# The beginning of a hybrid decoder block: a weight piece in four transfers, norm weights turned on TensorE, transposes by halves between matmuls

## Chip, cores and metric

One core of a Trainium2 chip runs the kernel. The metric is the device time of one execution in microseconds; lower is better. The kernel before was timed in three runs, the median is 810.13 us.

## What is computed

The block takes 512 tokens of 1024 float32 features. The part that matters here is its first step: an RMS norm with weights `norm1_g`, then one projection with `w_in` into 4096 columns.

```python
h = rmsnorm(x, norm1_g)          # x * rsqrt(mean(x*x) + EPS) * g
proj = h @ w_in                  # (512, 1024) @ (1024, 4096)
u, q, k, v, gate_p, gate_a = columns of proj
x = x + (sigmoid(gate_p) * pool_mixer(u) @ w_pool_up
         + sigmoid(gate_a) * diff_attention(q, k, v) @ w_attn_up) @ w_out
x = x + hier_moe(rmsnorm(x, norm2_g))   # top 1 of 4 groups, top 2 of 8 experts in it, 32 SwiGLU experts
```

The expert weights are by far the largest input: 32 experts of three 1024 x 512 float32 matrices.

## The kernel before, in words

**Tiles.** The 512 tokens are four tiles of 128. `w_in` is cut into pieces of 512 rows by 512 columns (1 MB, four chunks of 128 rows, `k` = 0 to 3). Pieces 0 and 1 are the two row halves of the query columns, 2 and 3 those of the key columns, and so on. A product at the precision wanted is three matmuls: high part by high part, high by low and low by high. So every weight chunk is split by `split_to` (lines 149 to 167): ScalarE multiplies the chunk by the norm weights and rounds it to the high part `wh` (line 159), VectorE forms the rest `wl` (line 160). The activations are treated in the same way: `h_transpose` (line 257) transposes the normed token tile on TensorE into the PSUM tile `tx` (line 262, 128 columns at a time), ScalarE copies it to the high part `hTh` (line 265), VectorE forms `hTl` (line 266). Half 0 of `hT` belongs to the first 512 features and so to even pieces, half 1 to odd ones.

**A unit.** `tok_unit` (line 270) is one piece by one token tile: for each of four chunks the matmuls of lines 274, 275 and 276, twelve in all. It can call a function after a chunk (`mid`).

**Order.** The schedule is written out by hand: each engine carries out its instructions in the order in which the program issues them, and waits only on what it reads or overwrites. The beginning is lines 466 to 485. First twelve matmuls of the identity (line 469, tile `warm`) keep TensorE busy while x arrives. Then `h_norm` of tiles 0 and 1 (sum of squares on ScalarE, line 250; mean plus EPS on VectorE, line 252; power -0.5 on GpSimd, line 188; scaling on VectorE, line 254), the transposes of tile 0, two chunks split, `h_norm(2)`, two more chunks, the transposes of tile 1, `h_norm(3)`. Then comes the first loop of four units on piece 0; behind units 0 and 1 stand the transposes of tiles 2 and 3, and behind units 2 and 3 the splits of the four chunks of piece 1. After that `late_consts` (line 227) works out small tables on VectorE (the ALiBi bias in four parts on line 229, and lines 230 to 241), with one exponential on ScalarE in the midst (line 240) that reads what VectorE made on line 238. A second loop runs four units on piece 1, which are the first to read half 1 of `hT`; from then on `tick` splits chunks ahead by a fixed lead.

**Transfers.** Nearly all loads are issued by SyncE (SP) in program order. At the beginning: x tiles 0 and 1, the norm weights `g1c` (line 172: element by element, 1024 of 4 bytes, so that they lie down the partitions), weight piece 0 (line 146), x tiles 2 and 3, weight piece 1, then small constants and later pieces as buffers come free. The expert weights come last and fill most of the second half; the transfers that start them wait for buffers that earlier stages release.

Of the kernel before, what the change touches and what calls it, by code (L numbers as in the profile page):

```python
# [10 lines left out]
F32 = mybir.dt.float32  # L11
# [6 lines left out]
OP = mybir.AluOpType  # L18
# [4 lines left out]
NT, ND = SEQ // 128, D // 128  # L23
# [27 lines left out]
def hybrid_block_kernel(  # L51
# [27 lines left out]
    nc = tc.nc  # L79
# [5 lines left out]
    const = ctx.enter_context(tc.tile_pool(name="const", bufs=1))  # L85
# [10 lines left out]
    def S(shape, dt=F32, name="s"):  # L96
        return big.tile(shape, dt, tag="S", name=f"{name}{next(names)}")
# [7 lines left out]
    def bank(name="b", shape=(128, 512)):  # L105
        return psum.tile(list(shape), F32, tag="B", name=f"{name}{next(names)}")

    def small(shape, tag, dt=F32, bufs=3):
        return tiny.tile(shape, dt, tag=tag, name=f"{tag}{next(names)}", bufs=bufs)
# [6 lines left out]
    def f(ap):  # L116
        return ap.bitcast(F32)
# [4 lines left out]
    def x_tile(t):  # L122
        return xt[t // 2][:, t % 2, :]

    def load_x(t):
        nc.sync.dma_start(x_tile(t), x_rows[t * 128:(t + 1) * 128, :])
# [14 lines left out]
    def stage_to(n):  # L141
        while n_loaded[0] < min(n, len(pieces)):
            i = n_loaded[0]
            w, k0, c0 = pieces[i]
            st = S([128, 4, 512], name="w")
            nc.sync.dma_start(st, w[k0 * 128:(k0 + 4) * 128, c0:c0 + 512].rearrange("(k p) c -> p k c", p=128))
            staged[i] = st
            n_loaded[0] += 1

    def split_to(n):  # L150
        while n_split[0] < min(n, 4 * len(pieces)):
            i, c = divmod(n_split[0], 4)
            if c == 0:
                stage_to(i + 1)
                ready[i] = (S([128, 4, 512], F32R, name="wh"), S([128, 4, 512], F32R, name="wl"))
            src, hi, lo = staged[i][:, c, :], ready[i][0][:, c, :], ready[i][1][:, c, :]
            if pieces[i][0] is w_in:
                g = g1c[:, pieces[i][1] + c:pieces[i][1] + c + 1]
                nc.scalar.mul(hi, src, g)  # L159
                stt(lo, src, g, f(hi), op0=OP.mult, op1=OP.subtract)  # L160
            else:
                nc.scalar.copy(hi, src)
                tt(lo, src, f(hi), op=OP.subtract)
            if c == 3:
                del staged[i]
                stage_to(i + STG)
            n_split[0] += 1

    g1c = const.tile([128, ND], F32, name="g1c")
    load_x(0)  # L170
    load_x(1)
    nc.sync.dma_start(g1c, bass.AP(tensor=norm1_g.tensor, offset=norm1_g.offset, ap=[[1, 128], [128, ND]]))
    stage_to(1)
    for t in range(2, NT):
        load_x(t)
    stage_to(2)

# [3 lines left out]
    ident = const.tile([128, 128], F32, name="ident")  # L181
# [5 lines left out]
    def rsqrt(r, ms):  # L187
        nc.gpsimd.tensor_tensor(r, ms, mhalf[:, :ms.shape[-1]], op=OP.pow)
# [13 lines left out]
    for i, v in enumerate((lambda_q1, lambda_k1, lambda_q2, lambda_k2)):  # L202
        nc.sync.dma_start(lam_v[:, i, :], bcast(v, HD))
    nc.sync.dma_start(cols[:, 0:4], bass.AP(tensor=pool_scale.tensor, offset=pool_scale.offset,
                                            ap=[[1, 128], [128, 4]]))
# [21 lines left out]
    def late_consts():  # L227
        for h in range(H):
            ts(bias4[:, h, :], dist, -(2.0 ** (-8.0 * (h + 1) / H)), None, op0=OP.mult)
        nc.vector.reciprocal(rc, rc)  # L230
        nc.vector.tensor_copy(ident_h, ident)
        tt(wr, wr, g2c[:, :, None].to_broadcast([128, ND, NG + NE]), op=OP.mult)
        ts(qk_g[:, 0:1], qk_g[:, 0:1], HD ** -0.5, None, op0=OP.mult)
        ts(cols[:, 4:5], cols[:, 4:5], 1.0 - LAM_INIT, None, op0=OP.mult)
        lsum = const.tile([128, 2], F32, name="lsum")
        lscr = T("lscr")[:, :HD]
        for i in range(2):
            stt(lscr, lam_v[:, 2 * i, :], 1.0, lam_v[:, 2 * i + 1, :], op0=OP.mult, op1=OP.mult,
                accum_out=lsum[:, i:i + 1])
        nc.scalar.activation(lsum, lsum, AF.Exp)  # L240
        stt(neglam, lsum[:, 1:2], -LAM_INIT, lsum[:, 0:1], op0=OP.add, op1=OP.subtract)


    hT = [(S([128, 4, SEQ], F32R, name="hTh"), S([128, 4, SEQ], F32R, name="hTl")) for _ in range(2)]
    rst = const.tile([128, NT], F32, name="rst")

    def h_norm(t):
        xn = S([128, 2, D], name="xn")
        ss = small([128, 1], "ss")
        nc.scalar.activation(xn[:, 1, :], x_tile(t), AF.Square, accum_out=ss)  # L250
        ms = small([128, 1], "ms")
        ts(ms, ss, 1.0 / D, EPS, op0=OP.mult, op1=OP.add)
        rsqrt(rst[:, t:t + 1], ms)
        nc.vector.tensor_scalar(xn[:, 0, :], x_tile(t), rst[:, t:t + 1], None, op0=OP.mult)
        return xn

    def h_transpose(t, xn):
        for half in range(2):
            p = bank("tx", (128, 4, 128))
            for j in range(4):  # L260
                c = half * 4 + j
                nc.tensor.transpose(p[:, j, :], xn[:, 0, c * 128:(c + 1) * 128], ident)
            hi, lo = hT[half]
            s = slice(t * 128, (t + 1) * 128)
            nc.scalar.copy(hi[:, :, s], p)
            tt(lo[:, :, s], p, f(hi[:, :, s]), op=OP.subtract)


    def tok_unit(b, i, kh, t, src, first, last, mid={}):
        whi, wlo = ready[i]  # L270
        ahi, alo = src[kh]
        s = slice(t * 128, (t + 1) * 128)
        for k in range(4):
            mm(b, ahi[:, k, s], whi[:, k, :], start=first and k == 0, stop=False)
            mm(b, ahi[:, k, s], wlo[:, k, :], start=False, stop=False)
            mm(b, alo[:, k, s], whi[:, k, :], start=False, stop=last and k == 3)
            if k in mid:
                mid[k]()
# [187 lines left out]
    bq = [bank("q") for _ in range(NT)]  # L466
    warm = bank("warm", (128, 4, 128))
    for j in range(WARM):
        mm(warm[:, j % 4, :], ident, ident, start=True, stop=True)
    xn = [h_norm(0), h_norm(1)]  # L470
    h_transpose(0, xn[0])
    split_to(2)
    xn.append(h_norm(2))
    split_to(4)
    h_transpose(1, xn[1])
    xn.append(h_norm(3))
    for t in range(NT):
        tok_unit(bq[t], 0, 0, t, hT, True, False)
        unit_no[0] += 1
        if t + 2 < NT:  # L480
            h_transpose(t + 2, xn[t + 2])
        else:
            split_to(4 + 2 * (t - 1))
    late_consts()
    split_to(8)

# [504 lines left out]
    def take(w, e, part):  # L991
        return [ew.pop((w, e + par, part)) for par in range(2)]
# [101 lines left out]
    for p in range(n_pair):  # L1094
# [38 lines left out]
        if last_pair:  # L1133
            y = bank("y")
            w = take("h", e, 0)
            for j in range(4):
                for par in range(2):
                    r = slice(par * CAP, (par + 1) * CAP)
# [12 lines left out]
        halves = [take("d", e, half) for half in range(2)]  # L1151
# [37 lines left out]
```

## Time and profile before

| | |
|---|---|
| median of 3 runs | 810.13 us (809.83 to 811.2) |
| the profiled execution's own time | 808.41 us |
| its span, first to last instruction | 806.2 us |
| mean granted TensorE clock | 0.995 |
| TensorE matmul busy | 777.3 us, 96% of the span |
| VectorE, ScalarE, GpSimd busy | 360.4, 203.9, 69.6 us |

The profile is of one execution. The timeline lists instructions by start; "x4" merges a run of four of the same kind, and then the second number is the whole stretch. A bracket says how long the engine sat idle before the row, and what ended that. Matmul rows are pipelined, so the start of one to the start of the next tells the pace, not the length of a row. PEld is the weight load of TensorE, DVE is VectorE, ACT ScalarE, POOL GpSimd, SP SyncE. The granted clock is a share of full speed (2.4 GHz).

### The profile page before, as it was taken

Reading aid. Unit: us, or ns where it says so; the run is one execution under the profiler, and the core shown is the slowest. Engines: PE = TensorE matmul, PEld = TensorE weight load, DVE = VectorE, ACT = ScalarE, POOL = GpSimd, SP = SyncE. Lnnn points to the kernel's source line nnn. Section 1 sums busy time; section 2 is a strip of 40 time slices with the busy share of each in tenths; the row PEclk is TensorE's granted clock in tenths of the full one; section 3 lists DMA queues with packets and bytes.
Section 4 is the critical chain, followed back from the end, with each engine's and each line's share of the span. In section 5 each row is a group of like instructions: output and inputs, shape, how many; then the busy total and the mean of one; then the engine's idle time right before and its main releaser. Section 6 shows DMA issues by size and latency. Waiting matters only on the chain. (4 is left out here: it accounts for less than half of the span.)

```text
span 806.2 us, 9635 instructions
## 1 busy us (share of the span) xinstructions
PE 777.3 (96%) x3686; PEld 450.9 (56%) x3686; DVE 360.4 (45%) x848; ACT 203.9 (25%) x390; POOL 69.6 (9%) x85
## 2 busy tenths in 40 slices
PE   7999999999999999999999989999999999999897
PEld 6888777778888888734444434434334334334334
DVE  5644486655463724556453243425225225224215
ACT  5644445454633424420100001000000000000001
POOL 1221060000100001001000000000000000000000
PEclk9999999999999999999999999999999999999999
DMA  9431111123138673999999959999999999999996
GB/s 323 128 100 53 52 53 56 57 98 105 54 119 298 234 289 135 387 399 425 425 426 426 426 221 425 428 424 426 426 426 427 426 426 427 425 427 426 426 418 241
DMA packets 55711, 240.07 MB, mean 298 GB/s; under 512 B 11176, under 2 KB 14760, under 8 KB 32112
## 3 DMA queue, kind: packets, MB, share of 16 engines
q1 hardware_dynamic: 52928, 233.37, 72.1%
q0 software_dynamic: 2736, 6.07, 1.9%
q8 instruction: 30, 0.49, 0.2%
q14 instruction: 17, 0.14, 0.0%
HBM read 239.13 MB, written 4.19 MB: 302 GB/s over the span
## 5 line engine op out<-in xcount | busy, mean ns | idle before, releaser
L923 PE MATMUL up<-e,xT 128*64 128x512 f32 x512 | 123.1, 595 | 11.5 <-DMA e<-in_w_expert_up_dram 11.3
L923 PE MATMUL gate<-e,xT 128*64 128x512 f32 x512 | 115.9, 603 | 4.5 <-DVEq L1054 3.0
L972 PE MATMUL y<-e,hT 128*64 128x512 f32 x480 | 116.0, 605 | 0.7 <-ACT hT L938 0.7
L929 DVE TENSOR_TENSOR h<-up,sg 128x512 f32<-128x512 f32 x16 | 17.2, 1076 | 190.5 <-PE up L923 190.5
L923 PEld LDWEIGHTS up<-e,xT 128*64 128x64 f32 x512 | 38.6, 137 | 92.5 <-issue 66.4
L923 PEld LDWEIGHTS gate<-e,xT 128*64 128x64 f32 x512 | 38.5, 138 | 73.2 <-issue 65.1
L988 DVE TENSOR_TENSOR acc<-sc,acc 128x512 f32<-128x512 f32 x124 | 76.8, 681 | 0.2
L972 PEld LDWEIGHTS y<-e,hT 128*64 128x64 f32 x480 | 34.9, 138 | 71.2 <-issue 63.7
L160 DVE SCALAR_TENSOR_TENSOR wl<-w,g1c,wh 128x512 fp32r<-128x512 f32 x64 | 48.9, 791 | 38.6 <-ACT wh L159 38.5
L285 PE MATMUL g<-hTh,wh 128*128 128x512 f32 x160 | 64.8, 405 | 0.2
L287 PE MATMUL g<-hTh,wl 128*128 128x512 f32 x160 | 62.4, 390 | 0.0
L286 PE MATMUL g<-hTl,wh 128*128 128x512 f32 x160 | 62.4, 390 | 0.0
L978 DVE SCALAR_TENSOR_TENSOR yl<-y,wv,yh 128x512 fp32r<-128x512 f32 x31 | 23.3, 750 | 77.4 <-ACT yh L977 74.7
L984 PE MATMUL sc<-yh,PT 128*128 128x512 f32 x124 | 53.2, 429 | 0.0
L977 ACT ACTIVATE yh<-y,wv 128x512 fp32r<-128x512 f32 x31 | 21.3, 688 | 119.8 <-PE y L972 115.6
L984 PE MATMUL sc<-yl,PT 128*128 128x512 f32 x124 | 48.9, 394 | 0.0
L938 ACT COPY hT<-ht 128x512 f32<-128x512 f32 x16 | 9.4, 587 | 151.8 <-PE ht L936 151.8
L159 ACT ACTIVATE wh<-w,g1c 128x512 fp32r<-128x512 f32 x64 | 44.6, 720 | 0.9 <-DMA w<-in_w_in_dram 0.9
L927 ACT ACTIVATE sg<-gate 128x512 f32<-128x512 f32 x16 | 9.6, 597 | 133.9 <-PE gate L923 133.9
L879 POOL MEMSET rows<- 128x1024 f32 x14 | 13.3, 952 | 347.5 <-PE xg L889 318.5
L984 PEld LDWEIGHTS sc<-yh,PT 128*128 128x128 f32 x124 | 23.3, 188 | 28.1 <-issue 24.7
L285 PEld LDWEIGHTS g<-hTh,wh 128*128 128x128 f32 x160 | 30.0, 188 | 13.2 <-issue 5.4
(228 smaller groups left out, 1088.6 us busy)
## 6 DMA issues: line engine op xcount, KB each, us to landing
e<-in_w_expert_gate_dram SPq DMA_DIRECT2D x64, 1024.0 KB, 19.8
e<-in_w_expert_down_dram SPq DMA_DIRECT2D x62, 1024.0 KB, 19.5
e<-in_w_expert_up_dram SPq DMA_DIRECT2D x60, 1024.0 KB, 20.2
w<-in_w_in_dram SPq DMA_DIRECT2D x16, 1024.0 KB, 5.6
w<-in_w_out_dram SPq DMA_DIRECT2D x4, 1024.0 KB, 4.9
e<-in_w_expert_up_dram SPq DMA_DIRECT2D x8, 512.0 KB, 14.1
x<-in_x_dram SPq DMA_DIRECT2D x4, 512.0 KB, 6.3
w<-in_w_pool_up_dram SPq DMA_DIRECT2D x2, 1024.0 KB, 4.9
```

Source lines behind the costliest of these rows:

```text
L159: nc.scalar.mul(hi, src, g)
L160: stt(lo, src, g, f(hi), op0=OP.mult, op1=OP.subtract)
L285: mm(b, whi[:, k, s], ahi[:, k, :], start=first and k == 0, stop=False)
L286: mm(b, whi[:, k, s], alo[:, k, :], start=False, stop=False)
L287: mm(b, wlo[:, k, s], ahi[:, k, :], start=False, stop=last and k == 3)
L923: mm(b[s, :], xs[par][:, j, :], w[par][:, k, :], start=j == 0, stop=j == 7)
L929: tt(h[:np_], bu[:np_].rearrange("p (q j) -> p j q", j=4), sg[:np_].rearrange("p (q j) -> p j q", j=4), op=OP.mult)
L972: mm(y[r, :], hTt[:, j, r], w[j // 2][par][:, j % 2, hf * 512:(hf + 1) * 512], start=j == 0, stop=j == 3)
L977: nc.scalar.mul(hi, y, wv)
L978: stt(lo, y, wv, f(hi), op0=OP.mult, op1=OP.subtract)
L984: mm(b, PT[:, t * 128:(t + 1) * 128], y2[k], start=k == 0, stop=k == 1)
L988: tt(a, b, a, op=OP.add)
```

## The change

- The first weight piece is loaded in four transfers of one chunk each. It now stands right behind x tile 0 and the norm weights; x tiles 1 to 3 follow it.
- The norm weights are loaded as eight rows of 128 (`g1r`), transposed on TensorE behind the identity matmuls, and copied to `g1c` by VectorE ahead of everything else of the beginning.
- `h_norm` is cut into `h_rstd` (the statistics) and `h_scale`. The scaling of tile 1 goes to ScalarE.
- The transposes go by halves: half 0 of tile 0 ahead of the first unit; half 0 of tile t+1 inside unit t behind its chunk 2; half 1 of tile t-1 inside unit t behind its chunk 0; half 1 of tile 3 behind unit 3.
- The statistics and scaling of tiles 2 and 3 move behind units 0 and 1.
- The chunks of piece 1 are split one behind each of units 1, 2 and 3; the fourth one stands behind `late_consts`.

```diff
--- before.py
+++ after.py
@@ -143,7 +143,11 @@
             i = n_loaded[0]
             w, k0, c0 = pieces[i]
             st = S([128, 4, 512], name="w")
-            nc.sync.dma_start(st, w[k0 * 128:(k0 + 4) * 128, c0:c0 + 512].rearrange("(k p) c -> p k c", p=128))
+            step = 1 if i == 0 else 4
+            for k in range(0, 4, step):
+                r = (k0 + k) * 128
+                nc.sync.dma_start(st[:, k:k + step, :],
+                                  w[r:r + step * 128, c0:c0 + 512].rearrange("(k p) c -> p k c", p=128))
             staged[i] = st
             n_loaded[0] += 1
 
@@ -167,11 +171,11 @@
             n_split[0] += 1
 
     g1c = const.tile([128, ND], F32, name="g1c")
+    g1r = const.tile([ND, 128], F32, name="g1r")
     load_x(0)
-    load_x(1)
-    nc.sync.dma_start(g1c, bass.AP(tensor=norm1_g.tensor, offset=norm1_g.offset, ap=[[1, 128], [128, ND]]))
+    nc.sync.dma_start(g1r, bass.AP(tensor=norm1_g.tensor, offset=norm1_g.offset, ap=[[128, ND], [1, 128]]))
     stage_to(1)
-    for t in range(2, NT):
+    for t in range(1, NT):
         load_x(t)
     stage_to(2)
 
@@ -244,18 +248,24 @@
     hT = [(S([128, 4, SEQ], F32R, name="hTh"), S([128, 4, SEQ], F32R, name="hTl")) for _ in range(2)]
     rst = const.tile([128, NT], F32, name="rst")
 
-    def h_norm(t):
+    def h_rstd(t):
         xn = S([128, 2, D], name="xn")
         ss = small([128, 1], "ss")
         nc.scalar.activation(xn[:, 1, :], x_tile(t), AF.Square, accum_out=ss)
         ms = small([128, 1], "ms")
         ts(ms, ss, 1.0 / D, EPS, op0=OP.mult, op1=OP.add)
         rsqrt(rst[:, t:t + 1], ms)
-        nc.vector.tensor_scalar(xn[:, 0, :], x_tile(t), rst[:, t:t + 1], None, op0=OP.mult)
         return xn
 
-    def h_transpose(t, xn):
-        for half in range(2):
+    def h_scale(t, xn, on_scalar=False):
+        r = rst[:, t:t + 1]
+        if on_scalar:
+            nc.scalar.mul(xn[:, 0, :], x_tile(t), r)
+        else:
+            nc.vector.tensor_scalar(xn[:, 0, :], x_tile(t), r, None, op0=OP.mult)
+
+    def h_transpose(t, xn, halves=(0, 1)):
+        for half in halves:
             p = bank("tx", (128, 4, 128))
             for j in range(4):
                 c = half * 4 + j
@@ -467,20 +477,30 @@
     warm = bank("warm", (128, 4, 128))
     for j in range(WARM):
         mm(warm[:, j % 4, :], ident, ident, start=True, stop=True)
-    xn = [h_norm(0), h_norm(1)]
-    h_transpose(0, xn[0])
-    split_to(2)
-    xn.append(h_norm(2))
+    gt = bank("g1t")
+    nc.tensor.transpose(gt[:, :ND], g1r, ident[:ND, :ND])
+    nc.vector.tensor_copy(g1c, gt[:, :ND])
+    xn = [h_rstd(0)]
+    h_scale(0, xn[0])
+    split_to(1)
+    xn.append(h_rstd(1))
+    h_transpose(0, xn[0], (0,))
+    split_to(3)
+    h_scale(1, xn[1], True)
     split_to(4)
-    h_transpose(1, xn[1])
-    xn.append(h_norm(3))
     for t in range(NT):
-        tok_unit(bq[t], 0, 0, t, hT, True, False)
+        mid = {}
+        if t > 0:
+            mid[0] = lambda: h_transpose(t - 1, xn[t - 1], (1,))
+        if t + 1 < NT:
+            mid[2] = lambda: h_transpose(t + 1, xn[t + 1], (0,))
+        tok_unit(bq[t], 0, 0, t, hT, True, False, mid)
         unit_no[0] += 1
         if t + 2 < NT:
-            h_transpose(t + 2, xn[t + 2])
-        else:
-            split_to(4 + 2 * (t - 1))
+            xn.append(h_rstd(t + 2))
+            h_scale(t + 2, xn[t + 2])
+        split_to(4 + t)
+    h_transpose(NT - 1, xn[NT - 1], (1,))
     late_consts()
     split_to(8)
 
```

## Rows read from the trace of the kernel before

**Rows 1.** The page: the chain that ended last, by engine, as shares of the span.

```profile
DMA 33%; PE 7%; DVE 0%; issue 0%; ACT 0%; DVEq 0%; SPq 0%; ACTq 0%
```

**Rows 2.** Stretches (us): length, each engine's busy time (instructions), granted clock, DMA share, GB/s.

```profile
10.00:15.00 5.00, 3.00 (x10) 1.67 (x10) 3.61 (x7) 5.00 (x9) 0.55 (x1) 1.00 1.05 399
...
26.00:320.00 294.00, 293.50 (x1393) 235.72 (x1392) 154.57 (x356) 134.84 (x270) 34.84 (x38) 1.00 0.34 121
```

**Rows 3.** Waits of the SP queue, 240 to 330: us in total, times, longest.

```profile
SPq L623 <- PE wo L276: 42.6, 4, 20.2
```

**Rows 4.** Timeline of all engines, the first 11 us: start us, length us.

```profile
1.75 5.08 PE L469 MATMUL warm<-ident 128*128 128x128 f32 x24 [1.75 <-DVE ident L182]
...
4.19 1.06 ACT L250 ACTIVATE xn<-x 128x1024 f32<-128x1024 f32 x1 [2.18 <-DMA x<-in_x_dram]
...
5.37 0.15 DVE L252 TENSOR_SCALAR ms<-ss 128x1 f32<-128x1 f32 x1 [3.67 <-ACT xn L250]
...
5.67 1.06 ACT L250 ACTIVATE xn<-x 128x1024 f32<-128x1024 f32 x1 [0.33 <-DMA x<-in_x_dram]
6.22 0.75 DVE L254 TENSOR_SCALAR xn<-x,rst 128x1024 f32<-128x1024 f32 x1 [0.69 <-POOL rst L188]
...
7.03 1.09 PE L262 MATMUL tx<-ident,xn 128*128 128x128 f32 x8 [0.19 <-DVE ms L252]
...
7.72 1.07 ACT L265 CAST hTh<-tx 128x512 fp32r<-128x512 f32 x2 [0.90 <-PE tx L262]
...
9.73 1.33 ACT L159 ACTIVATE wh<-w,g1c 128x512 fp32r<-128x512 f32 x2 [0.94 <-DMA w<-in_w_in_dram]
...
10.51 0.49 PE L274 MATMUL q<-wh,hTh 128*128 128x512 f32 x1 [0.90 <-ACT wh L159]
```

**Rows 5.** Timeline of PE, 15 to 29 us.

```profile
15.70 1.03 PE L262 MATMUL tx<-ident,xn 128*128 128x128 f32 x8
...
19.36 1.03 PE L262 MATMUL tx<-ident,xn 128*128 128x128 f32 x8
20.15 0.48 PE L274 MATMUL q<-wh,hTh 128*128 128x512 f32 x1
...
28.44 0.39 PE L274 MATMUL q<-wh,hTh 128*128 128x512 f32 x1
```

**Rows 6.** Timeline of ACT and DVE, 20 to 28 us.

```profile
20.00 1.08 ACT L265 CAST hTh<-tx 128x512 fp32r<-128x512 f32 x2 [2.58 <-PE tx L262]
...
20.61 1.29 DVE L266 TENSOR_TENSOR hTl<-tx,hTh 128x512 fp32r<-128x512 f32 x2 [1.71 <-ACT hTh L265]
20.95 2.57 ACT L159 ACTIVATE wh<-w,g1c 128x512 fp32r<-128x512 f32 x4
...
24.47 1.42 DVE L229 TENSOR_SCALAR bias<-dist 128x512 f32<-128x512 f32 x4
...
27.06 0.20 ACT L240 ACTIVATE lsum<-lsum 128x2 f32<-128x2 f32 x1 [3.54 <-DVE lscr L238]
```

**Rows 7.** Groups by line and shape, 0 to 30 us: count, busy us, mean ns.

```profile
L159 ACT ACTIVATE wh<-w,g1c 128x512 fp32r<-128x512 f32 x9 | 6.0, 719 | 0.9 <-DMA w<-in_w_in_dram 0.9
L160 DVE SCALAR_TENSOR_TENSOR wl<-w,g1c,wh 128x512 fp32r<-128x512 f32 x8 | 5.6, 745 | 0.8 <-ACT wh L159 0.8
L266 DVE TENSOR_TENSOR hTl<-tx,hTh 128x512 fp32r<-128x512 f32 x8 | 5.1, 683 | 1.7 <-ACT hTh L265 1.7
...
L265 ACT CAST hTh<-tx 128x512 fp32r<-128x512 f32 x8 | 4.3, 585 | 4.5 <-PE tx L262 4.5
```

**Rows 8.** Timeline of PE, 470 to 482 us.

```profile
473.08 0.39 PE L984 MATMUL sc<-yl,PT 128*128 128x512 f32 x1
476.43 5.78 PE L923 MATMUL gate<-e,xT 128*64 128x512 f32 x18 [2.95 <-DVEq L1054]
```

**Rows 9.** Stretches as in rows 2, around the wait of rows 8.

```profile
470.00:480.00 10.00, 7.05 (x28) 2.84 (x26) 4.04 (x9) 0.69 (x1) 0.00 (x0) 0.87 0.33 104
480.00:490.00 10.00, 10.00 (x48) 3.32 (x46) 0.00 (x0) 0.60 (x1) 0.00 (x0) 0.96 1.01 425
```

## The prediction

> **What bounds the kernel now.** I read the chain of waits first. A third of the span on it is expert weights in flight [rows 1]: the second half is a stream of transfers, each waiting for the one ahead. Then the stretches. Between 26 and 320 us TensorE (PE) is busy 293.5 of 294 us [rows 2], so this stretch is as long as its matmuls, and nothing can take up a delay handed to it. Then the waits of SP's queue: the early expert transfers waited 42.6 us in all for PE's matmuls of the output projection to release buffers [rows 3]. So the stream cannot start before PE gets there. A microsecond that PE gains or loses before 26 us moves the stream and, one for one, the end. The change is therefore read in the first 28 us alone, by one marker: the first matmul of the second unit on piece 1, at 28.44 us [rows 5].
>
> The beginning shows PE waiting. The identity matmuls run from 1.75 to 6.83 us, the transposes of tile 0 start at 7.03, but the first product comes at 10.51, behind a weight piece that reached ScalarE (ACT) at 9.73 [rows 4]. It is dense only from the transposes at 15.70 on [rows 5].
>
> **The change, part by part.**
>
> *Start.* Chunks of piece 0 now land early. Two x tiles of half a MB released ACT 1.48 us apart (4.19 and 5.67 [rows 4]), so a quarter MB is 0.74 us, and the first chunk is there at about 4.9. But no chunk can be split before `g1c` exists, and `g1c` comes out of a transpose that PE's queue holds behind the identity matmuls: 6.83. From the first of four transposes to the ACT copy is 0.69 us [rows 4]; at 0.10 per transpose (eight in 0.79, 19.36 to 20.15 [rows 5]) one alone is read 0.39 after its start, so the copy to `g1c` runs at 7.2, for 0.15 as a small VectorE (DVE) instruction does [rows 4]. It stands on DVE ahead of the mean of tile 0. That mean was ready to run at 5.37 and now runs at 7.35, with scaling, transposes and ACT's copy queued behind it: from mean to copy is 2.35 us (5.37 to 7.72 [rows 4]), so the copy can run at 9.7.
>
> Ahead of that copy on ACT now stands the square of tile 1. Its x lands behind a whole MB of weights: 4.19 + 3 x 1.48 = 8.63; with 1.06 for the square and 0.1 for its readout, ACT is free at 9.8. No row shows a load under this order; the bounds are no hold at all (9.7) and half a MB more in front (11.3), and I take 9.8, since 1.48 is this queue's own pace. The copy takes 0.585 [rows 7], the first product follows at 10.45. **Gain: 0.06 us.** The five microseconds by which the weights come earlier are spent waiting for the norm weights and x tile 1.
>
> *Unit 0.* ACT goes on with two chunks (0.62 apart, 2.57 less the last 0.72 over three [rows 6, 7]), the scaling of tile 1 (no such row on ACT; the square over the same 128x1024 takes 1.06, DVE's scaling 0.75 [rows 4]; I take 1.0 between starts, by the engine) and the fourth chunk: 9.8 + 0.50 + 1.24 + 1.0 = 12.55. High part 0.72, low part 0.745 [rows 7]: 14.1, and two products later unit 0 ends at 14.6. Before it ended at 15.70 [rows 5]. **Gain so far 1.1.**
>
> *Units 1 to 3.* Three units take 8.29 us (20.15 to 28.44 [rows 5]). Before, tiles 0 and 1 were transposed in PE's idle time ahead of 10.5. Now six half tiles are transposed within these units or behind them: 6 x 0.40 = 2.4. Each first half stands only one chunk (three matmuls, 0.69) ahead of its unit. From transposes to copy is 0.64 (19.36 to 20.00 [rows 5, 6]), the copy 0.585, while PE has 0.40 + 0.69 to do: 0.18 of wait, and 0.27 more for `hTl`, 0.68 long [rows 7]. Unit 1 is spared, since unit 0 ends late; units 2 and 3 pay 0.45 each. Sum 14.6 + 8.3 + 2.4 + 0.9 = 26.2; the second loop began at 28.44 - 2.76 = 25.7. **The gain is gone: 0.5 late.** The scalings of tiles 2 and 3 end on DVE just as PE wants them (about 17.0 and 21.0); if they are late, PE is too, at most 0.5 each.
>
> *Constants ahead of the last chunk.* Here is the main cost. The fourth chunk of piece 1 stands behind `late_consts`, which stands behind half 1 of tile 3. Before, all four chunks were split from 20.95 on and the constants followed at 24.47, under cover of PE's units [rows 6]. Now: transposes at 25.75, ACT's copy 0.64 later at 26.4, `hTl` 0.61 later at 27.0 (20.00 to 20.61), the constants 0.64 later at 27.65. From the bias to ACT's exponential is 2.59 us (24.47 to 27.06), the exponential 0.20 [rows 6]: `wh` of the chunk runs at 30.45, is read at 31.2. PE, with nine matmuls of 0.23 done since 26.2, wants it at 28.2: **3.0 lost**, and 0.55 more for `wl`, 0.745 long. The marker comes at 32.4 in place of 28.44. **Sum: 4.0 late**; 3.7 if x tile 1 holds nothing up.
>
> *The rest at nothing.* SP issues three transfers more, which push the small constants back; their first reader, `late_consts`, now runs 3.2 us later and covers that. The element-wise load goes away, but was awaited by nothing once the weights were later than it.
>
> **The clock.** A wait of 2.95 us in PE (473.47 to 476.43 [rows 8]) was followed by half speed: mean granted clock 0.87 over ten microseconds and 0.96 over the next, 1.3 + 0.4 = 1.7 us of work lost [rows 9]. The new wait is as long, with another 0.55 right behind it. Against it: 2.0 us idle out of 5 between 10 and 15 us left the clock at 1.00 [rows 2]. I take the row that is nearest in length: **1.7 us**, into a stretch that PE bounds; bounds 0 and 3.4 (the wait at the start, 6.9 to 8.9 and to 10.4, might do the same). The Trainium skill, "TensorE: Matmul & The Clock Gate", section "Why this matters for your kernels", tells authors to avoid long idle gaps between bursts of matmuls, since the clock goes back to half; the trace at 476 us agrees, and by it the sum is 5.7 rather than 4.0.
>
> **Sum.** 4.0 + 1.7 = 5.7 us on the profiled execution's 808.41 (span 806.2, 2.2 around it): 814.1. That execution lies 1.7 below the median of the runs, so against 810.13: **815.8 us**.
>
> **Rivals.**
> 1. *Delay without a drop of the clock.* 810.13 + 4.0 = 814.1 (813.8 at 3.7). Chance 0.36, the forecast 0.50.
> 2. *Slower still: quarters as dear as half MBs.* If each transfer costs 1.48 whatever its size, the fourth chunk lands at 10.1 and x tile 1 at 11.6; ACT's copy waits 3.0 longer, and the marker is 7.0 late: 817.1. The two equal x tiles cannot tell size from count, but 399 GB/s between 10 and 15 us speak for size [rows 2]. Chance 0.03. The Trainium skill, "DMA: Bandwidth & Descriptors", section "Bandwidth", has such a rule against this change: batch transfers to a MiB, as smaller ones reach less of the peak; no run here shows quarters.
> 3. *No change: the constants find cover.* If the fourth chunk does not wait for them, the 3.5 falls away and 0.5 late is left: 810.6. For it: nothing in the rows; it needs `late_consts` to be short or elsewhere. Chance 0.07.
> 4. *Faster: the queues do not keep the program's order.* Place: DVE at 5.4 us and ACT at 27. If the mean of tile 0 runs when ready, the start is 2.0 earlier, and if the last chunk passes the constants, 3.5 falls away: 4.0 - 2.0 - 3.5 = -1.5, and 808.6. Half of it (either alone) is not enough; that is its point of decision. Against it: all rows of the beginning stand in the program's order, ACT's splits at 20.95 ahead of its exponential at 27.06 among them [rows 4, 6]. Chance 0.04.
>
> **Numbers.** About 0.2% (1.6 us) is what a measurement here can tell from no change. Faster 0.04 (rival 4), same 0.07 (rival 3), slower 0.89 (forecast, rivals 1 and 2). The range reaches from 812.4 (rival 1 at 3.7, and 1.4 less, about the spread of the three runs) to 817.8 (forecast with 2.0 of its other bounds: x tile 1, late scalings, the second drop); it leaves out rivals 3 and 4.
>
> **What would show it.** Right: `g1c`'s copy at 7.2, the mean of tile 0 at 7.35, first product near 10.4; DVE's bias near 27.6, ACT's exponential with a wait of some 3 us, PE idle about 3 us before the fourth chunk of the second loop, marker at 32.4; granted clock under 1 behind it; PE dense from there to 320 as before. Wrong: a marker under 30, or the marker late and the first expert transfers not.

## The result, and the profile after

The changed kernel took 817.54 us (815.81 to 819.2, 4 runs) against 809.98: a ratio of 1.009 with a 95% interval of 1.0064 to 1.0116. It is 7.6 us slower; 5.7 was forecast, and 817.5 lies in the range of 812.4 to 817.8. The profiled execution took 815.81 us, with a span of 813.5 in place of 806.2.

The timeline of the changed kernel's first 11 us answers to [rows 4]:

```profile
1.75 5.49 PE L479 MATMUL warm<-ident 128*128 128x128 f32 x24 [1.75 <-DVE ident L186]
...
7.17 0.23 PE L481 MATMUL g1t<-ident,g1r 8*128 8x8 f32 x1
...
7.43 0.17 DVE L482 COPY g1c<-g1t 128x8 f32<-128x8 f32 x1 [5.74 <-PE g1t L481]
7.52 0.14 DVE L256 TENSOR_SCALAR ms<-ss 128x1 f32<-128x1 f32 x1
7.64 0.72 ACT L163 ACTIVATE wh<-w,g1c 128x512 fp32r<-128x512 f32 x1 [2.38 <-DVE g1c L482]
...
9.16 0.66 PE L272 MATMUL tx<-ident,xn 128*128 128x128 f32 x4 [1.76 <-DVE xn L265]
...
9.26 1.06 ACT L254 ACTIVATE xn<-x 128x1024 f32<-128x1024 f32 x1 [0.90 <-DMA x<-in_x_dram]
...
10.31 0.57 ACT L275 CAST hTh<-tx 128x512 fp32r<-128x512 f32 x1
...
10.93 0.80 PE L284 MATMUL q<-wh,hTh 128*128 128x512 f32 x1 [1.11 <-ACT hTh L275]
```

To see: VectorE (DVE) stood 5.74 us in front of the copy to `g1c`, since TensorE (PE) reaches the transpose of the norm weights only behind the identity matmuls. The mean of tile 0, ready at 5.3, ran at 7.52. ScalarE's (ACT) first copy to `hTh` then had to let the square of x tile 1 go first (9.26). Where the kernel before had its first product at 10.51, this one has it at 10.93, though the weights' first chunk was there for the split at 7.64.

PE's timeline further on, answering to [rows 5]:

```profile
15.81 0.50 PE L284 MATMUL q<-wh,hTh 128*128 128x512 f32 x1
...
19.98 0.50 PE L284 MATMUL q<-wh,hTh 128*128 128x512 f32 x1
...
27.73 0.60 PE L272 MATMUL tx<-ident,xn 128*128 128x128 f32 x4
28.08 0.48 PE L284 MATMUL q<-wh,hTh 128*128 128x512 f32 x1
...
33.04 0.50 PE L284 MATMUL q<-wh,hTh 128*128 128x512 f32 x1 [2.63 <-ACT wh L163]
33.83 0.50 PE L285 MATMUL q<-wl,hTh 128*128 128x512 f32 x1 [0.28 <-DVE wl L164]
...
34.40 0.52 PE L284 MATMUL q<-wh,hTh 128*128 128x512 f32 x1
```

And the rows of ACT and DVE that made it wait, answering to [rows 6]:

```profile
28.36 0.59 ACT L275 CAST hTh<-tx 128x512 fp32r<-128x512 f32 x1 [1.31 <-PE tx L272]
...
28.98 0.69 DVE L276 TENSOR_TENSOR hTl<-tx,hTh 128x512 fp32r<-128x512 f32 x1 [1.14 <-ACT hTh L275]
29.59 1.42 DVE L233 TENSOR_SCALAR bias<-dist 128x512 f32<-128x512 f32 x4
...
32.17 0.20 ACT L244 ACTIVATE lsum<-lsum 128x2 f32<-128x2 f32 x1 [3.23 <-DVE lscr L242]
32.28 0.70 ACT L163 ACTIVATE wh<-w,g1c 128x512 fp32r<-128x512 f32 x1
```

This is the chain that was forecast, row by row: transposes of tile 3's half, `hTh`, `hTl`, constants, exponential, and only then the fourth chunk of piece 1, for which PE waited. The clock shows in the stretches, which answer to [rows 2, 9] (the seventh number is the granted clock):

```profile
10.00:15.00 5.00, 4.07 (x14) 3.23 (x15) 2.94 (x5) 3.76 (x7) 0.56 (x1) 0.66 1.02 382
26.00:320.00 294.00, 290.58 (x1361) 232.43 (x1360) 155.55 (x347) 133.83 (x270) 33.64 (x36) 0.99 0.33 117
33.00:38.00 5.00, 4.68 (x12) 3.52 (x13) 1.72 (x4) 2.91 (x5) 1.65 (x1) 0.66 0.00 0
```

Between 10 and 15 us the granted clock was 1.00 before [rows 2] and is 0.66 now: half of full speed (1.2 for 2.4 GHz) in two thirds of the stretch, behind PE's waits of 1.76 and 1.11 us. It falls again behind the wait at 30 us. What is lost by the end of the new wait goes through to the end, as the start of the expert stream shows:

The end of unit 0 in the changed kernel is the start of its last product, 15.43, and one pace of 0.23. Forecast is by how much later the prediction has each row.

| us | before | after | later by | forecast |
|---|---|---|---|---|
| first product | 10.51 | 10.93 | 0.4 | -0.1 |
| last product of unit 0 done | 15.70 | 15.66 | 0.0 | -1.1 |
| second loop begins | 25.72 | 28.08 | 2.4 | 0.5 |
| marker, second unit of the second loop | 28.44 | 34.40 | 6.0 | 4.0 |
| ACT reads that unit's result | 31.45 | 38.94 | 7.5 | 5.7 |
| first expert transfer issued | 261.16 | 268.85 | 7.7 | 5.7 |
| span | 806.2 | 813.5 | 7.3 | 5.7 |

### The profile page after: what moved, and what is told of

Read it like the earlier page. It is cut to its first block, busy times and chain, and to the rows that moved or that the text cites. A ratio compares the mean times of both kernels' runs of the same rounds, so it can differ in the third digit from the quotient of the medians.

```text
span 813.5 us, 9641 instructions
## 1 busy us (share of the span) xinstructions
PE 782.3 (96%) x3687; PEld 452.5 (56%) x3687; DVE 360.7 (44%) x848; ACT 205.5 (25%) x391; POOL 69.5 (9%) x85
```

## The experiments

All kernels compute the whole block. Each ratio is to runs of the kernel before on the same chip (medians 810.28, 809.78 and 809.90 us in the three sessions: runs e1 to e4, e5 to e8, e9 to e12).

**e1_chunk_first: the last chunk ahead of the constants.**

```diff
         split_to(4 + t)
+    split_to(8)
     h_transpose(NT - 1, xn[NT - 1], (1,))
     late_consts()
-    split_to(8)
```

> The changed kernel with one line moved: the fourth chunk of piece 1 is split ahead of the last half transposes and of the constants. Theory (the chunk waits behind the constants, and the half-speed stretch follows from that wait): PE no longer waits before the fourth chunk of the second loop, 2.79 us and 0.56 us fall away, and so does the stretch at half speed behind it (1.7 us); the marker comes at 31.0 instead of 34.4 us; time 817.5 - 5.1 = 812.4 us. Rival A (the half transposes and their waits are the cost, the constants only showed it): less than 1 us faster, over 816.5. Rival B (the half-speed stretch has another cause, such as the one at 10 us): only the 3.4 us go, 814.1.

813.27 us, ratio 1.0038 (1.0025 to 1.0050): 4.3 less than the changed kernel's 817.54, between the theory and rival B. The wait is gone, and with it the half speed behind it:

```profile
8.00:10.00 2.00, 0.97 (x4) 0.57 (x4) 0.70 (x2) 0.48 (x1) 0.00 (x0) 0.57 1.02 412
10.00:15.00 5.00, 3.80 (x9) 2.99 (x10) 2.94 (x5) 4.03 (x7) 0.56 (x1) 0.50 0.90 335
30.00:40.00 10.00, 10.00 (x47) 8.26 (x46) 7.23 (x23) 6.22 (x13) 1.88 (x2) 1.00 0.30 104
```

Rival A falls. But 3 us over the kernel before are left where my sum has 0.5, and the first two rows show a suspect: half speed at the beginning, here for nearly 7 us, while the changed kernel's profile has it for 3.4 (0.66 over five microseconds).

**e2_before_chunk_last: that order alone, in the kernel before.**

```diff
-            split_to(4 + 2 * (t - 1))
+            split_to((6, 7)[t - 2])
```

> The kernel before with only this taken over: the fourth chunk of piece 1 is split behind the constants. Theory (the order costs because in the changed kernel the constants stand behind half 1 of the last token tile, which comes out of PE only after unit 3; by itself the order is nearly covered): the constants run from about 23.8, the exponential at 26.4, the chunk's high part at 26.7, its low part ready at 28.1 against 28.0 wanted: at most 0.3 us slower, 810.0 to 810.3. Rival (constants ahead of the chunk cost 3 us wherever they stand): 813 or more.

809.65 us, ratio 0.9994 (0.9980 to 1.0008): nothing. In its profile the chunk does stand behind the exponential:

```profile
30.17 0.20 ACT L240 ACTIVATE lsum<-lsum 128x2 f32<-128x2 f32 x1 [3.49 <-DVE lscr L238]
30.28 0.71 ACT L159 ACTIVATE wh<-w,g1c 128x512 fp32r<-128x512 f32 x1
```

yet PE's only wait between 22 and 330 us is one of 0.3 in the attention. So the order of these two lines costs nothing by itself that the runs can tell (the interval leaves 0.6 us). With e1 this says that it costs once the constants stand behind a transpose that PE does after its last unit.

**e3_fill: work for PE in the new wait.**

```diff
+    def fill(n):
+        for j in range(n):
+            mm(warm2[:, j % 4, :], ident, ident, start=True, stop=True)
+
+    warm2 = bank("warm", (128, 4, 128))
     for t in range(NT):
-        tok_unit(bq[t], 1, 1, t, hT, False, True)
+        tok_unit(bq[t], 1, 1, t, hT, False, True, {2: lambda: fill(12)} if t == 0 else {})
```

> The changed kernel with twelve more identity matmuls on PE behind the third chunk of the first unit of the second loop, where PE waits 2.79 us; their result is not used. At 0.11 us for each of their 24 records (the pace of matmuls of this shape late in the kernel) they take 2.6 us and fit into the wait. Theory (PE's idleness brings the half-speed stretch): granted clock 1.00 from 34 to 38 us, 1.7 us faster, 815.8. Rival (the stretch follows from something else than idleness): clock as before, 817.5 or a little more.

816.67 us, ratio 1.0082 (1.0062 to 1.0102): 0.9 less than the changed kernel, half of what was expected, and within the spread of both. In the profile the fill lies in the wait and the clock stays up:

```profile
31.34 2.84 PE L513 MATMUL warm<-ident 128*128 128x128 f32 x24
```

```profile
34.00:40.00 6.00, 5.72 (x25) 4.41 (x24) 2.64 (x5) 4.40 (x9) 1.65 (x1) 1.00 0.00 0
```

**e4_one_transfer: the first piece in one transfer.**

```diff
-            step = 1 if i == 0 else 4
+            step = 4
```

> The changed kernel with the first weight piece in one transfer again, at the same place in the queue. Theory (the early chunks are of no use, since all four splits wait for the norm weights at 7.6 us and for ACT, which stands behind x tile 1): no change, 817.5, within 1 us. Rival A (quarters are dear: 300 GB/s from 3 to 6 us in the changed kernel): x tile 1 lands earlier than 9.26, by some 0.5 to 0.8 us, and the marker moves by that, 816.8. Rival B (early chunks matter): the first chunk's split comes after 7.64 and the time grows by up to 1 us.

817.55 us, ratio 1.0094 (1.0074 to 1.0115): no change, as the theory had it. In the profiled execution the first split waited for the piece until 9.44, not for the norm weights, and still the first product (12.29) waited for ACT's copy behind x tile 1, not for weights:

```profile
9.44 0.72 ACT L163 ACTIVATE wh<-w,g1c 128x512 fp32r<-128x512 f32 x1 [4.17 <-DMA w<-in_w_in_dram]
...
10.62 1.06 ACT L254 ACTIVATE xn<-x 128x1024 f32<-128x1024 f32 x1 [0.46 <-DMA x<-in_x_dram]
```

x tile 1 did not land earlier than with quarters: 10.62 here, 8.95 to 9.69 in the seven profiled executions with quarters in the same place (the changed kernel, e1, e3, e5, e9, e10, e11). That is one execution against seven, and the interval of the time is 1.7 us to either side, so rival A's 0.7 has nothing for it but is not excluded by the time.

**e5_fill_start: work for PE at the beginning of e1.**

```diff
...
+    fill(7)
     h_transpose(0, xn[0], (0,))
+    fill(4)
     split_to(3)
```

> e1_chunk_first with eleven more identity matmuls where its PE waits at the beginning: seven ahead of the transposes of tile 0, four behind them (1.5 and 0.9 us at full pace, in waits of 1.8 and 2.1 us); their results are not used. Theory (in e1 the half speed from 8 to 15 us comes from these waits and makes most of what e1 still loses to the kernel before): granted clock 1.00 from 8 to 15 us, first product at the same time within 0.3 us, 1.5 to 2.5 us faster than e1: 811. Rival A (the loss is the half transposes and the waits for them, and the clock only slows work that waits anyway): 813.3 as e1. Rival B (the fill runs at half pace itself and holds up the transposes): up to 2 us slower than e1.

`fill` is that of e3, on the tile `warm`. 811.55 us, ratio 1.0019 (1.0008 to 1.0031): 1.7 less than e1 in their medians, and 1.2 less when each is taken against the kernel before in its own session. The fill took 0.13 us for each record, and the clock held:

```profile
7.35 1.83 PE L482 MATMUL warm<-ident 128*128 128x128 f32 x14
```

```profile
10.00:15.00 5.00, 4.84 (x24) 3.22 (x23) 3.38 (x6) 4.52 (x9) 0.56 (x1) 1.00 0.88 328
```

The first product came at 10.62, for 11.20 in e1, because x tile 1 landed 0.6 us earlier; that is not the fill's doing. From there to the second loop PE takes 16.2 us (10.62 to 26.86), for 17.5 in e1 (11.20 to 28.74): 1.3 less. So the half speed at the beginning is worth 1.2 to 1.7 us, although PE waits in the same stretch. Both rivals fall: e5's slowest execution, 812.98, is below e1's median.

**e6_x1_first: x tile 1 and the mean of tile 0 first.** On e1; the statistics of tile 1 also move ahead of the first split, so that ACT squares x tile 1 before it waits for the norm weights:

```diff
     load_x(0)
+    load_x(1)
     nc.sync.dma_start(g1r, ...)
     stage_to(1)
-    for t in range(1, NT):
+    for t in range(2, NT):
...
-    nc.vector.tensor_copy(g1c, gt[:, :ND])
     xn = [h_rstd(0)]
     h_scale(0, xn[0])
-    split_to(1)
     xn.append(h_rstd(1))
+    nc.vector.tensor_copy(g1c, gt[:, :ND])
+    split_to(1)
```

> e1_chunk_first with x tile 1 loaded right behind x tile 0, ahead of the norm weights and of piece 0, and with the copy to the norm weights on VectorE moved behind the scaling of tile 0. Theory (the early weights are wasted because the mean of tile 0 stands behind that copy, and ACT's first copy behind x tile 1): mean at 5.4, transposes of tile 0 at 7.2, ACT's copy no later than 8.2, first product between 8.9 and 9.8 instead of 11.2, shorter waits in PE, and 1 to 3 us faster than e1: 810.3 to 812.3. Rival (the weights are then what is late, since they land behind one MB of x): first product still past 10.5, and 813.3 as e1.

809.41 us, ratio 0.9992 (0.9982 to 1.0003): 3.9 less than e1 in their medians (3.4 against each session's kernel before), more than expected, level with the kernel before. The copy to `g1c` is as late as ever, but nothing of tile 0 stands behind it:

```profile
5.28 0.15 DVE L257 TENSOR_SCALAR ms<-ss 128x1 f32<-128x1 f32 x1 [3.58 <-ACT xn L255]
...
7.44 0.17 DVE L486 COPY g1c<-g1t 128x8 f32<-128x8 f32 x1 [0.49 <-PE g1t L482]
```

```profile
8.88 0.49 PE L285 MATMUL q<-wh,hTh 128*128 128x512 f32 x1 [0.90 <-ACT hTh L276]
```

The first product is at 8.88, and in this profile the granted clock stays at 1.00 through the beginning.

**e7_before_early_g: the kernel before with the loading side alone.** Quarters and the transposed norm weights, x tiles 0 and 1 first, the copy to `g1c` behind the mean of tile 1:

```diff
...
-    nc.sync.dma_start(g1c, ...)
+    nc.sync.dma_start(g1r, ...)
     stage_to(1)
...
-    xn = [h_norm(0), h_norm(1)]
+    gt = bank("g1t")
+    nc.tensor.transpose(gt[:, :ND], g1r, ident[:ND, :ND])
+    xn = [h_norm(0), h_norm(1, lambda: nc.vector.tensor_copy(g1c, gt[:, :ND]))]
```

> The kernel before with only the loading side of the change, in a better order: piece 0 in four transfers, the norm weights as rows, transposed on PE behind the identity matmuls and copied by VectorE behind the mean of tile 1; x tiles 0 and 1 stay first in the queue, whole-tile transposes and splits as before. Theory (the second half follows the beginning one for one; the late first piece and the element-wise load cost the kernel before its wait at 9.7 us): the first product at 9.4 instead of 10.5 and the marker 1 us earlier: 809.2, against 810.2. Rival A (the wait for the low part of chunk 2 absorbs it): same, 810.2. Rival B (more than that, since the kernel before also falls to half speed in some executions and would no longer): 808 or less.

809.34 us, ratio 0.9991 (0.9980 to 1.0001). The size is that of the theory, but the interval touches 1, so it isn't settled. In its profile the first product came 1.3 us earlier, at 9.23, and chunk 2 then made PE wait 1.15 us for its low part, as in the kernel before. Behind that the clock fell:

```profile
15.00:21.00 6.00, 6.00 (x28) 5.12 (x27) 2.71 (x6) 1.23 (x3) 0.55 (x1) 0.72 1.01 339
```

**e8_early_halves: halves a unit ahead of their use.** On e7, with whole calls between the units and none inside:

```diff
...
-    h_transpose(0, xn[0])
+    h_transpose(0, xn[0], (0,))
     split_to(2)
-    xn.append(h_norm(2))
+    h_transpose(1, xn[1], (0,))
     split_to(4)
-    h_transpose(1, xn[1])
-    xn.append(h_norm(3))
+    xn.append(h_norm(2))
+    h_transpose(0, xn[0], (1,))
...
-        if t + 2 < NT:
-            h_transpose(t + 2, xn[t + 2])
-        else:
-            split_to(4 + 2 * (t - 1))
+        if t == 0:
+            xn.append(h_norm(3))
+            h_transpose(2, xn[2])
+            h_transpose(1, xn[1], (1,))
+        elif t == 1:
+            split_to(5)
+            h_transpose(3, xn[3])
+            split_to(6)
+        elif t == 2:
+            split_to(8)
```

> e7_before_early_g with transposes by halves, but a whole unit ahead of their use and outside the units: half 0 of tiles 0 and 1 and half 1 of tile 0 ahead of the first unit, tile 2 and half 1 of tile 1 behind unit 0, tile 3 behind unit 1, splits of piece 1 done by the end of unit 2. Theory (halves as such cost nothing; what costs is to use a half one chunk after its transposes, and the order of the constants): 0.2 us faster than e7, 809.0. Rival (halves cost by themselves, through more switches between kinds of matmuls): 0.5 us or more slower than e7.

808.21 us, ratio 0.9978 (0.9967 to 0.9989): faster than both kernels, 1.6 us under the one before and 1.1 under e7, where 0.2 was expected. The rival falls. Of PE's waits behind the identity matmuls 1.6 us are left for scalings and 0.3 for a low part:

```profile
PE tx L269 <- DVE xn L261: 1.6, 2, 0.8
PE qk L335 <- DVE yTl L453: 0.3, 1, 0.3
PE q L282 <- DVE wl L164: 0.3, 1, 0.3
```

No run isolates the surplus over the 0.2. The profiles show two candidates: e7's wait of 1.15 for a low part, and the clock, which is 1.00 here where e7 fell:

```profile
15.00:21.00 6.00, 6.00 (x34) 5.09 (x33) 4.83 (x8) 4.11 (x9) 0.23 (x1) 1.00 1.07 363
```

**e9_changed_again: the changed kernel, six more executions.** No edit.

> The changed kernel as it is, again, with more executions and beside the next three on one chip. Theory: 817.5 us again, within 1, and a profile with half speed at the beginning and behind the wait for the fourth chunk. Rival (the first four executions were on a chip with longer transfers): 815 or less.

816.55 us (814.59 to 820.43), ratio 1.0093 (1.0071 to 1.0115), within 1 us of the theory; the rival falls. The profiled one is the fastest of the six: half speed from 8.7 to 15.5 us, but none behind the wait at 30 us, which is as long as ever:

```profile
30.00:40.00 10.00, 7.09 (x30) 5.32 (x29) 5.98 (x21) 5.32 (x10) 1.65 (x1) 1.00 0.29 105
```

So the second fall comes in some executions and not in others: it is in the profiles of the changed kernel and of e4, not in this one. That fits the wide spread of this kernel, and e3's half gain; it also means that e3's profile alone does not show that the fill held the clock.

**e10_both_fills: the changed kernel with the fills of e3 and e5.** The edits are those two.

> The changed kernel with the identity matmuls of e3_fill and those of e5_fill_start, 23 in all, so that PE is not idle in either wait. Theory (the delay by order stays, the clock's share goes): granted clock 1.00 from 8 to 40 us, e9_changed_again less 1.7 at the beginning and 0.9 to 1.7 behind the wait: 814.0 to 815.0, which leaves 4 to 5 us over the kernel before, the 4.0 of the sum without the clock. Rival (the clock is paid in work that waits anyway): within 1 us of e9.

814.60 us, ratio 1.0058 (1.0039 to 1.0076): 2.0 less than e9, and 4.7 over the kernel before, as in the theory; the intervals of e9 and e10 overlap at their edges. The clock is at 1.00 in both places:

```profile
10.00:12.00 2.00, 0.95 (x5) 0.42 (x4) 0.81 (x3) 2.00 (x5) 0.56 (x1) 1.00 1.02 405
...
33.00:38.00 5.00, 4.71 (x21) 3.87 (x21) 1.75 (x5) 3.90 (x8) 1.65 (x1) 1.00 0.02 9
```

The fills held nothing up. The transposes of tile 0 start 1.98 us behind that of the norm weights (1.99 in the changed kernel), and the product behind the second fill 3.03 us behind the last one ahead of it (3.02). From the first product to the second loop PE takes 16.2 us, as in e5:

```profile
11.36 0.50 PE L284 MATMUL q<-wh,hTh 128*128 128x512 f32 x1 [1.04 <-ACT hTh L275]
...
27.57 0.48 PE L284 MATMUL q<-wh,hTh 128*128 128x512 f32 x1
```

In e9 it takes 17.9 (10.87 to 28.73). What the change costs by its order alone is thus 4.7 us (0.58%, 0.39 to 0.76).

**e11_copy_behind: the copy's place alone, on e1.** Of e6 only the copy's move behind the scaling; x tile 1 and its square stay where e1 has them.

```diff
-    nc.vector.tensor_copy(g1c, gt[:, :ND])
     xn = [h_rstd(0)]
     h_scale(0, xn[0])
+    nc.vector.tensor_copy(g1c, gt[:, :ND])
```

> e1_chunk_first with the copy to the norm weights on VectorE behind the scaling of tile 0, and x tile 1 left behind the weights. It parts the two edits of e6_x1_first. Theory (ACT's copy then still stands behind the square of x tile 1, which lands at 9.3 to 9.6): the transposes of tile 0 come at 7.2, but the first product only at 10.9 to 11.2, and the time is that of e1, 813.3, within 0.7. Rival (the wait for the copy was the cost, and the place of x tile 1 none): 809.4 to 810.5 as e6.

813.54 us, ratio 1.0047 (1.0031 to 1.0064), as e1. The transposes come 1.8 us earlier than in the changed kernel, and ACT's copy none:

```profile
7.38 0.78 PE L272 MATMUL tx<-ident,xn 128*128 128x128 f32 x4
...
10.75 0.54 PE L284 MATMUL q<-wh,hTh 128*128 128x512 f32 x1 [2.59 <-ACT hTh L275]
```

So two waits stood side by side, and removing one is worth nothing while x tile 1 is late. Whether x tile 1 first would do without the copy's move, and what the earlier square of tile 1 adds, no run shows.

**e12_halves_one_transfer: e8 with the first piece in one transfer.** The edit is that of e4.

> e8_early_halves with the first weight piece in one transfer. Theory (here, unlike in the changed kernel, the first chunk is what the first product waits for: x tile 0 and the norm weights are ready by 8.2): the piece lands at about 9.2 instead of chunk by chunk from 8, the first product comes at 10.0 to 10.3 instead of 9.3, and it is 0.7 to 1 us slower than e8: 809.0. Rival (quarters land no earlier or cost the queue as much): as e8, 808.2.

809.04 us, ratio 0.9984 (0.9972 to 0.9996). The first product is at 10.22, behind the weights, in place of 9.34:

```profile
9.45 1.33 ACT L163 ACTIVATE wh<-w,g1c 128x512 fp32r<-128x512 f32 x2 [1.27 <-DMA w<-in_w_in_dram]
```

The medians differ from e8 by 0.8, as expected, but the ratios by 0.5 us, and their intervals overlap: the first product's 0.9 us is shown, in one profile of each, the gain in time is not settled. The same four transfers that were worth nothing in the changed kernel (e4) bring the first product forward where the weights are what comes last.

## Why the prediction was right, and where its sum was short

**What bounds the kernel.** Right. PE is dense from the second loop on, and 7.5 us lost by 39 us were 7.7 at the first expert transfer and 7.3 at the end. All fourteen profiles bear it out: the first expert transfer is issued anywhere from 260.0 to 270.7 us, and the end comes 544.4 to 546.1 us behind it.

**Start.** The mechanism was right: the mean of tile 0 behind the copy (7.52 for 7.35), ACT's copy behind x tile 1. x tile 1 landed at 9.26 where I had 8.63 from the pace of 1.48 us per half MB, and it was later than 8.63 in all seven profiles with this order (8.95 at the earliest), so that term was too small. With it the first product came at 10.93, not 10.45. The copy's wait stands close behind: transposes at 9.16 and 0.69 more to ACT's copy [rows 4] make 9.85, against 10.31. e11 moved the copy alone and gained nothing; e6 took away both waits and gained 3.9 us.

**Unit 0.** Here a step failed. I had taken the wait at the start as harmless to the clock by the row nearest to it, 2.0 us idle out of 5 at 1.00 [rows 2], and put half speed there into the bounds only. It came in all six profiled executions that load x tile 1 behind the weights and have no fill at the start (the changed kernel, e1, e3, e4, e9, e11), and in neither of the two with the fill (e5, e10). From the first product to the second loop PE takes 16.2 us at full clock (e5, e10), 17.15 in the changed kernel, 17.5 in e1 and 17.9 in e9: a price of 0.9, 1.3 and 1.7 us. Unit 0 itself takes 4.24 us in e10, where I had 4.15, and 4.73 in the changed kernel. So of the 1.1 us that it should have gained, half went to the late first product and half to the clock.

**Units 1 to 3.** The sum had 11.6 us from the end of unit 0 to the second loop, the profile has 12.4 (15.66 to 28.08), and at full clock it is 12.0 (e10, 15.61 to 27.57). The first matmul behind each set of transposes takes 0.31 to the next, not 0.23 (28.08 to 28.39 in the changed kernel), five times over; that was missed. That unit 1 is spared was right at full clock (e5, e10). In the changed kernel it waits for its half too, because the slow unit 0 runs through its fourth chunk without the wait for the low part (0.17 in e10) that lets the half's copies catch up.

Together these terms (0.5 for x tile 1, 0.9 for the clock at the start, 0.45 for the matmuls behind transposes) are the 1.9 us by which the second loop came later than the sum had it, 28.08 for 26.2. They use up nearly all of the 2.0 us that the range kept above the forecast: 817.5 lies 0.3 under its end.

**Constants ahead of the last chunk.** Right in place and size: waits of 2.8 and 0.56 (from 30.02 + 0.23 to 33.04; 33.83 less 33.04 less 0.23) where I had 3.0 and 0.55. e1 takes them away, with 4.3 us; e2 shows that it needs the transposed half in front of the constants.

**The clock behind the wait.** It fell as the row at 476 us suggested [rows 8, 9]: 0.66 on average from 33 to 38 us, 1.7 lost in five microseconds. But it is a matter of the execution: without a fill there it fell in two of three profiles (the changed kernel and e4, not e9), with one in neither (e3, e10). The Trainium skill's advice in "TensorE: Matmul & The Clock Gate", section "Why this matters for your kernels", is to avoid long idle gaps between bursts. The runs agree in so far as the clock stayed at 1.00 in every wait that was filled with idle matmuls (e3, e5, e10); they also show a fall behind the shorter waits of the start (1.76 and 1.11 us) and none behind the long one in e9. What I had wrong is that the term belongs to both waits, with a chance for each, and that both together come to about 2.0 us in the medians (e9 to e10), not 1.7 for one.

**Rivals.** Rival 1 (delay without a fall of the clock, 814.1) is what e10 brings about: 814.6. Rival 2 falls by the changed kernel's own row: x tile 1 landed at 9.26, not at 11.6. Rival 3 was the kernel without the wait, and e1 shows that this alone does not reach "no change": 3.0 us are left, of which the clock at the start is 1.2 to 1.7 (e5), and the late x tile 1 with the copy most of the rest (e6 is level with the kernel before). Rival 4 falls by the rows: both queues kept the program's order.

Summed up from the runs: the order alone 4.7 us (e10), the clock about 2.0 (e9 less e10), together the 6.7 of e9 over its kernel before; most of the 4.7 is the wait for the fourth chunk (2.8 and 0.56).

## What to carry to other kernels

Before moving a load forward, list what else its first reader waits for: four early chunks were worth nothing while the norm weights and another tile came later, and brought the first product forward by 0.9 us once they came last (in time perhaps 0.5 to 0.8, not settled). When a late piece of work is moved behind a loop, look at what the program puts behind it on each queue: here a block of constants, harmless before, came to stand between a transpose and a weight chunk. And price a wait of TensorE in a dense stretch with the half speed that may follow it, not with its length alone.

## What was not expected of the hardware

- The same identity matmuls, 24 records on an idle PE at the start, took 4.31 us in one execution and 5.49 in others (e4; the changed kernel), up to 0.23 us each, although the granted clock reads 1.00 from the first microsecond; 14 of them at 7.35 us in e5 took 1.83, 0.13 each. So the rows of the clock do not show the slow beginning, and the transpose of the norm weights, queued behind, moved between 5.99 (e4) and 7.18 us (e11) from one execution to another.
- The half speed at the beginning lasted 3.4 us in one execution of the changed kernel, and close to 7 in another (e9) with the same program. The kernel before is not free of it: e2's profile, which has its beginning, shows half speed from 14 to 21 us, behind a first piece that landed at 11.20 instead of 9.73, and issues the first expert transfer 4.1 us later (265.24 for 261.16). Of the kernel before's own executions beside the experiments, the six fastest (807.9 to 808.3 us) have a mean granted clock of 0.995, the six slowest (812.0 to 812.7) one of 0.990 to 0.992. A single profile of this beginning is worth up to four microseconds of doubt.
